# A 32-byte pad in front of the arena of a two-layer decoder trunk

## The chip, the cores and the metric

The kernel runs on one NeuronCore of one Trainium2 chip. The metric is the device time of one execution in microseconds (us), the median of several runs. The kernel before takes 2490.14 us (median of 3 runs, 2489.68 to 2490.35).

## What is computed

Two layers of a hybrid decoder trunk over 512 tokens of width 1024, all in float32. Each layer has three sub-layers with residual adds, each behind an RMSNorm: a parallel token mixing of four branches, a cross-attention with 4 heads into 256 memory tokens, and a gated MLP with a causal convolution of width 3. Cut to what matters:

```python
for l in range(DEPTH):                       # 2 layers
    h = rms_norm(x, mix_norm_g[l])
    seg_a, seg_b, seg_c, seg_d, seg_g = split_last(h @ w_in[l], SEGMENTS)   # 1024 x 9984
    y_a, y_b, y_c, y_d = dilated(seg_a), diff(seg_b), hgrn(seg_c), rwkv(seg_d)
    gates = jax.nn.sigmoid(seg_g.reshape(B, S, 4, D))
    merged = sum(gates[:, :, n] * (y_n @ p_n[l]))        # n = a, b, c, d
    x = x + merged @ w_mix_out[l]
    hq = rms_norm(x, mem_q_norm_g[l]) @ w_mem_q[l]
    kv = rms_norm(mem, mem_kv_norm_g[l]) @ w_mem_kv[l]
    p = jax.nn.softmax(hq @ k.T / 16)                    # 4 heads of 256
    x = x + (p @ v) @ w_mem_o[l]
    u = rms_norm(x, ffn_norm_g[l]) @ w_ffn_in[l]         # 1024 x 5632
    gate, val = jnp.split(causal_conv3(u), 2, axis=-1)
    x = x + (jax.nn.silu(gate) * val) @ w_ffn_out[l]     # 2816 x 1024
return rms_norm(x, final_norm_g)
```

## The kernel before, in words

**Numbers in two halves.** Every large product runs in fp32r, a float32 type of the matmul, with each operand cut into a rounded part (hi) and the rest (lo). One product of a 128x128 block is three matmuls that add up in PSUM (`mm3`): hi by hi, hi by lo, lo by hi. All of them are issued at L288, so the trace tells them apart by the names of their tiles. In a name like `ffn_pd<-xgh,whi`, `ffn_pd` is the PSUM tile written, the first name behind the arrow is the moving operand (streamed through the array) and the second is the stationary one (loaded ahead as weights, the LDWEIGHTS of the trace).

**Weights.** All weights come as 388 chunks of 128x1024 floats, 194 in each layer. `chunk` (from L473) loads one with a DMA from SP's queue into `wst`, rounds it to `whi` on ScalarE (L483) and subtracts on VectorE to get `wlo` (L484). There are 3, 4 and 4 buffers of these three.

**Kinds of fp32r matmul.** Four of them matter here:

- *weight-stationary, 512 columns* (`ws_tile`, `ws_run`): a 128x128 block of `whi` or `wlo` is stationary, 512 tokens of an activation move. 168 of a layer's 194 chunks are used so, with 8 blocks of 3 matmuls each: 2 x 168 x 24 = 8064 matmuls. They are the projections (`Cp_pd`, `Dp_pd`, `Bp_pd`, `A_pd`), the gates (`ga_pd` to `gd_pd`), the branch outputs (`pa_pd` to `pd_pd`), `mix_pd`, `mq_pd`, `mo_pd` and the MLP (`ffn_pd`). Per layer, the MLP has 66 chunks of them and `mix`, `mq` and `mo` 8 each, so that 2 x 90 x 24 = 4320 of the 8064 belong to these four.
- *weight-moving, 256 columns* (`tm_tile`): an activation is stationary and 256 columns of weights move: 18 chunks of each layer, four matmul rows of 128 tokens (two for `mv`), 1344 matmuls in all (`Cp_pd<-whi,xgh`, `Bp_pd<-whi,xgh`, `A_pd<-whi,xgh`, `mv_pd<-whi,mgh` and their lo forms).
- *memory keys, 256 columns* (`mk_pd`): weights stationary, 256 memory tokens moving, 384 matmuls.
- *cross-attention* (`matt_ps`): scores of 256 columns (`matt_ps<-mkh,mqh`, 192 matmuls) and the product of probabilities with values at 512 columns (`matt_ps<-mpth,mvh`, 96 matmuls). Here both operands are activations.

The other matmuls (mixers, transposes) are plain float32.

**Where the operands lie.** SBUF is cut into pools that lie one behind the other in each partition: `cp` (constants), `wp` (weights), `sp` (small and temporary tiles), `ar` (the arena). In the built program `cp` begins at byte 16512, `wp` at 33952, `sp` at 79008 and `ar` at 113792. Every buffer of `wp` (`wst`, `whi`, `wlo`) starts at a byte that is 32 above a multiple of 64, and so does every 128-column block of it, since a block is 512 bytes long. The arena has 15 slots of 4 KB and 25 of 2 KB and hands them out through `Arena.alloc`; 113792 is a multiple of 64, so every slot starts at byte 0 of a 64-byte line, and every block of 128 or 256 columns in it as well. All fp32r activations (`xgh`, `xgl`, `fh`, `fl`, `moh`, `mhh`, `mgh`, `mkh`, `mqh`, `mpth`, `mvh` and the like) lie in the arena, nearly all of `sp` at byte 32.

**Order of work.** `Weave` writes out, while the program is built, one fixed order for each engine: a queue of dense weight products, and chains of the mixers' steps that are put in between when a model of TensorE's time says that their inputs should be ready. `setup` (L607) runs first: it makes the constant `ones`, loads the first constants and `x`. The MLP has no chains beside it.

Of the kernel before, what the change touches and what calls it, by code (L numbers as in the profile page):

```python
# [9 lines left out]
F32 = mybir.dt.float32  # L10
# [11 lines left out]
P = 128  # L22
# [351 lines left out]
class Trunk:  # L374
# [232 lines left out]
    def setup(self):  # L607
        nc = self.nc
        self.ones = self.cp.tile([P, P], F32, name='ones')
        nc.vector.memset(self.ones, 1.0)  # L610
        nc.scalar.copy(self.ones[:, 0:2], self.ones[:, 2:4])
        self.load_cv(0)
        xg, acc = self.load_x()
        self.cst = self.cp.tile([P, NCS], F32, name='cst')
        nc.scalar.dma_start(self.cst, self.ins['cst'])
        return xg, acc
# [1385 lines left out]
```

## Time and profile before

| | before |
|---|---|
| median of 3 runs | 2490.14 us (2489.68 to 2490.35) |
| the profiled execution | 2490.42 us |
| its span, first to last instruction | 2488.6 us |
| TensorE matmul busy | 2439.0 us (98%), 13344 instructions |
| TensorE weight load busy | 1996.5 us (80%) |
| VectorE busy | 1513.4 us (61%) |
| ScalarE busy | 973.4 us (39%) |
| GpSimd busy | 455.6 us (18%) |
| mean granted TensorE clock | 0.995 of full speed |

Busy time is the union of an engine's instructions. A matmul's record in the trace is longer than the distance to the next one, because neighbours overlap: a 512-column matmul lasts some 0.40 us on record, but a new one starts every 0.23 us. What a stream of matmuls costs is therefore read from the starts, not from the mean duration.

### The profile page before, as it was taken

Reading aid. Unit: us, or ns where it says so; the run is one execution under the profiler, and the core shown is the slowest. Engines: PE = TensorE matmul, PEld = TensorE weight load, DVE = VectorE, ACT = ScalarE, POOL = GpSimd, SP = SyncE. Lnnn points to the kernel's source line nnn. Section 1 sums busy time; section 2 is a strip of 40 time slices with the busy share of each in tenths; the row PEclk is TensorE's granted clock in tenths of the full one; section 3 lists DMA queues with packets and bytes.
Section 4 is the critical chain, followed back from the end, with each engine's and each line's share of the span. In section 5 each row is a group of like instructions: output and inputs, shape, how many; then the busy total and the mean of one; then the engine's idle time right before and its main releaser. Section 6 shows DMA issues by size and latency. Waiting matters only on the chain.

```text
span 2488.6 us, 34307 instructions
## 1 busy us (share of the span) xinstructions
PE 2439.0 (98%) x13344; PEld 1996.5 (80%) x13344; DVE 1513.4 (61%) x2729; ACT 973.4 (39%) x1728; POOL 455.6 (18%) x374
## 2 busy tenths in 40 slices
PE   8999999999999999999999999999999999999997
PEld 7877887788889888888888788867888898888886
DVE  6787447756656566366466864387466565763762
ACT  6242524443334434234352335244333354432441
POOL 0220042244010111011102200433421001110112
PEclk9999999999999999999999999999999999999998
DMA  5224233224324122222322342332343332222221
GB/s 182 100 103 144 89 115 127 73 68 156 125 96 151 64 93 93 93 93 94 127 93 78 110 144 79 121 106 77 100 133 114 101 127 77 93 93 97 98 85 60
DMA packets 89602, 259.69 MB, mean 104 GB/s; under 512 B 18144, under 2 KB 21856, under 8 KB 89440
## 3 DMA queue, kind: packets, MB, share of 16 engines
q1 hardware_dynamic: 57168, 205.81, 25.0%
q10 hardware_dynamic: 25872, 30.58, 3.7%
q0 software_dynamic: 6400, 21.11, 2.7%
q8 instruction: 105, 1.72, 0.3%
q14 instruction: 57, 0.47, 0.1%
HBM read 234.32 MB, written 23.13 MB: 103 GB/s over the span
## 4 chain that ended last, share of the span: by engine, by line
PE 92%; DVE 5%; ACT 1%; issue 1%; DMA 1%; POOL 0%; DVEq 0%; ACTq 0%; SPq 0%
PE ffn_pd L288 30%; PE A_pd L288 7%; PE Bp_pd L288 5%; PE gc_pd L288 4%; PE Cp_pd L288 4%; PE gd_pd L288 4%; PE mq_pd L288 4%; PE mo_pd L288 4%; PE mix_pd L288 4%; PE ga_pd L288 4%; PE Dp_pd L288 3%; PE Db_ps L288 3%; PE gb_pd L288 2%; PE matt_ps L288 2%; PE mk_pd L288 2%; PE mv_pd L288 2%
## 5 line engine op out<-in xcount | busy, mean ns | idle before, releaser
L483 ACT CAST whi<-wst 128x1024 fp32r<-128x1024 f32 x388 | 405.3, 1049 | 830.5 <-PE ffn_pd L288 236.5
L484 DVE TENSOR_TENSOR wlo<-wst,whi 128x1024 fp32r<-128x1024 f32 x388 | 497.1, 1285 | 213.5 <-ACT whi L483 212.3
L288 PE MATMUL ffn_pd<-xgh,whi 128*128 128x512 f32 x704 | 278.8, 396 | 0.0
L288 PE MATMUL ffn_pd<-xgh,wlo 128*128 128x512 f32 x704 | 278.4, 395 | 0.0
L288 PE MATMUL ffn_pd<-xgl,whi 128*128 128x512 f32 x704 | 278.4, 395 | 0.0
L1866 POOL TENSOR_TENSOR ffn_ft<-ffn_ft,ffn_fc 128x512 f32<-128x512 f32 x44 | 60.1, 1366 | 563.0 <-DVE ffn_fu L1852 362.5
L288 PEld LDWEIGHTS ffn_pd<-xgh,wlo 128*128 128x128 f32 x704 | 132.2, 188 | 32.1
L288 PEld LDWEIGHTS ffn_pd<-xgl,whi 128*128 128x128 f32 x704 | 132.3, 188 | 31.9
L288 PEld LDWEIGHTS ffn_pd<-xgh,whi 128*128 128x128 f32 x704 | 132.3, 188 | 31.6
L288 PE MATMUL ffn_pd<-fh,wlo 128*128 128x512 f32 x352 | 139.2, 396 | 0.0
L288 PE MATMUL ffn_pd<-fh,whi 128*128 128x512 f32 x352 | 139.2, 396 | 0.0
L288 PE MATMUL ffn_pd<-fl,whi 128*128 128x512 f32 x352 | 139.2, 396 | 0.0
L288 PE MATMUL A_pd<-xgh,whi 128*128 128x512 f32 x256 | 106.9, 417 | 0.0
L288 PE MATMUL A_pd<-xgh,wlo 128*128 128x512 f32 x256 | 102.3, 399 | 0.0
L288 PE MATMUL A_pd<-xgl,whi 128*128 128x512 f32 x256 | 102.2, 399 | 0.0
L1853 DVE TENSOR_TENSOR ffn_fu<-ffn_pd,r_rbc 128x512 f32<-128x512 f32 x88 | 60.4, 688 | 57.6 <-PE ffn_pd L288 57.6
L531 DVE TENSOR_TENSOR fl<-ffn_ft,fh 128x512 fp32r<-128x512 f32 x44 | 30.5, 693 | 90.5 <-ACT fh L530 90.5
L530 ACT CAST fh<-ffn_ft 128x512 fp32r<-128x512 f32 x44 | 27.3, 621 | 144.1 <-POOL ffn_ft L1866 144.1
L1855 ACT ACTIVATE ffn_fc<-ffn_fu,cvt 128x512 f32<-128x512 f32 x88 | 71.7, 817 | 25.4 <-DVE ffn_fu L1853 25.4
L1415 POOL TENSOR_TENSOR A_rp<-A_rp,snr 128x512 f32<-128x512 f32 x24 | 50.4, 2098 | 167.4 <-DVE A_rp L1414 165.1
L288 PEld LDWEIGHTS ffn_pd<-fh,wlo 128*128 128x128 f32 x352 | 66.1, 188 | 16.1
L288 PEld LDWEIGHTS ffn_pd<-fl,whi 128*128 128x128 f32 x352 | 66.1, 188 | 16.0
(583 smaller groups left out, 6106.0 us busy)
## 6 DMA issues: line engine op xcount, KB each, us to landing
wst<-in_wst_dram SPq DMA_DIRECT2D x388, 512.0 KB, 3.5
gb_gate<-gb_gu ACTq DMA_DIRECT2D x16, 256.0 KB, 2.1
gd_gate<-gd_gu ACTq DMA_DIRECT2D x16, 256.0 KB, 2.1
gc_gate<-gc_gu ACTq DMA_DIRECT2D x16, 256.0 KB, 2.1
pc_gu<-gc_gate POOLq DMA_DIRECT2D x16, 256.0 KB, 3.6
pd_gu<-gd_gate POOLq DMA_DIRECT2D x16, 256.0 KB, 3.0
pb_gu<-gb_gate POOLq DMA_DIRECT2D x16, 256.0 KB, 3.1
x<-in_x_dram ACTq DMA_DIRECT2D x13, 256.0 KB, 3.4
```

The lines of the kernel that those rows point to most:

```text
L288: return self.te.matmul(out, lhsT, rhs, **kw)
L483: nc.scalar.copy(hi, st)
L484: nc.vector.tensor_sub(lo, st, hi.bitcast(F32))
L530: nc.scalar.copy(dst[0], src)
L531: nc.vector.tensor_sub(dst[1], src, dst[0].bitcast(F32))
L1415: nc.gpsimd.tensor_mul(t2, t2, self.snr)
L1853: nc.vector.tensor_mul(u[:, 2:514], ps, self.rb)
L1855: nc.scalar.activation(acc, u[:, 2:514], AF.Identity, scale=self.cv('cw2', ch), bias=self.cv('cb', ch))
L1866: nc.gpsimd.tensor_mul(th, th, cc[1])
```

## The change

A tile of 8 floats in each partition (32 bytes), `pad`, is taken from the pool `sp` before any other tile of it, and set to zero once on VectorE.

```diff
     def setup(self):
         nc = self.nc
         self.ones = self.cp.tile([P, P], F32, name='ones')
+        pad = self.sp.tile([P, 8], F32, name='pad')
+        nc.vector.memset(pad, 0.0)
         nc.vector.memset(self.ones, 1.0)
         nc.scalar.copy(self.ones[:, 0:2], self.ones[:, 2:4])
         self.load_cv(0)
```

In the built program every other tile of `sp` and every slot of `ar` lies 32 bytes higher than before, and no tile of `cp` or `wp` moves. The arena begins at byte 113824, so its slots start at byte 32 of a 64-byte line, as `wst`, `whi` and `wlo` do; nearly all of `sp` now starts at byte 0. The order of the instructions on every engine, and what each waits for, stay as they were, with one MEMSET of 128x8 more on VectorE at the very start.

## Rows read from the trace of the kernel before

**Rows 1.** The page: span, TensorE's busy time (share, instructions), granted clock in 40 slices.

```profile
span 2488.6 us, 34307 instructions
...
PE 2439.0 (98%) x13344; PEld 1996.5 (80%) x13344; DVE 1513.4 (61%) x2729; ACT 973.4 (39%) x1728; POOL 455.6 (18%) x374
...
PEclk9999999999999999999999999999999999999998
```

**Rows 2.** The page: shares by engine of the chain of work that ended last.

```profile
PE 92%; DVE 5%; ACT 1%; issue 1%; DMA 1%; POOL 0%; DVEq 0%; ACTq 0%; SPq 0%
```

**Rows 3.** Pieces of that chain in order of time: start us, us, what.

```profile
321.38 67.20 PE Bp_pd L288 x384
...
661.80 44.80 PE mix_pd L288 x192
...
753.18 22.72 PE mk_pd L288 x192
789.59 14.01 PE mv_pd L288 x120
...
883.25 358.39 PE ffn_pd L288 x1536
```

**Rows 4.** TensorE in order of time, MLP of layer 0: start us, us, operation.

```profile
1143.49 0.40 PE L288 MATMUL ffn_pd<-xgh,whi 128*128 128x512 f32 x1
1143.72 0.40 PE L288 MATMUL ffn_pd<-xgl,whi 128*128 128x512 f32 x1
1143.95 0.40 PE L288 MATMUL ffn_pd<-xgh,wlo 128*128 128x512 f32 x1
```

**Rows 5.** The same view, cross-attention of layer 0, probabilities by values.

```profile
803.43 0.40 PE L288 MATMUL matt_ps<-mpth,mvh 128*128 128x512 f32 x1
803.67 0.40 PE L288 MATMUL matt_ps<-mptl,mvh 128*128 128x512 f32 x1
803.90 0.39 PE L288 MATMUL matt_ps<-mpth,mvl 128*128 128x512 f32 x1
804.13 0.39 PE L288 MATMUL matt_ps<-mpth,mvh 128*128 128x512 f32 x1
...
806.17 0.28 PE L288 MATMUL matt_ps<-mkh,mqh 128*128 128x256 f32 x1
```

**Rows 6.** The same view, same place in layer 1.

```profile
2032.92 0.39 PE L288 MATMUL matt_ps<-mpth,mvh 128*128 128x512 f32 x1
...
2034.96 0.28 PE L288 MATMUL matt_ps<-mkh,mqh 128*128 128x256 f32 x1
```

**Rows 7.** The same view, scores of the cross-attention of layer 0.

```profile
826.13 0.28 PE L288 MATMUL matt_ps<-mkh,mqh 128*128 128x256 f32 x1
...
827.09 0.29 PE L288 MATMUL matt_ps<-mkh,mql 128*128 128x256 f32 x1
```

**Rows 8.** TensorE's waits: waiting line, releaser, us in total, times, longest.

```profile
PE Bb_ps L292 <- DVE bp L1497: 14.5, 13, 1.9
PE Cp_pd L288 <- ACT xgh L533: 9.8, 1, 9.8
PE Db_ps L292 <- DVE dsq L1048: 4.9, 2, 2.6
```

**Rows 9.** Groups of VectorE: line, operation, shapes, count, then busy us and mean ns.

```profile
L484 DVE TENSOR_TENSOR wlo<-wst,whi 128x1024 fp32r<-128x1024 f32 x388 | 497.1, 1285 | 213.5 <-ACT whi L483 212.3
L531 DVE TENSOR_TENSOR fl<-ffn_ft,fh 128x512 fp32r<-128x512 f32 x44 | 30.5, 693 | 90.5 <-ACT fh L530 90.5
L531 DVE TENSOR_TENSOR mhl<-mrg,mhh 128x512 fp32r<-128x512 f32 x16 | 10.7, 688 | 1.6 <-ACT mhh L530 1.4
L1852 DVE MEMSET ffn_fu<- 128x2 f32 x88 | 5.3, 60 | 0.0
```

**Rows 10.** Stretches: us, busy time (instructions) of PE, PEld, DVE, ACT, POOL, clock, DMA.

```profile
883.00:1241.60 358.60, 358.60 (x1540) 288.74 (x1539) 210.63 (x306) 133.94 (x168) 40.18 (x31) 1.00 0.31 101
```

## The prediction, made before the changed kernel was run

> **What bounds the kernel now.** I read the page first, then the chain of waits, then TensorE in order of time. The page shows TensorE busy for 2439.0 of 2488.6 us, at full clock (2.4 GHz) but for the last slice [rows 1], and 92% of the chain that ended last is TensorE [rows 2]. What it waits for is small: the three largest waits sum to 29 us [rows 8]. So the time is a number of matmuls times the distance between their starts, and a change that moves only addresses can act in one way that matters: by changing that distance.
>
> The chain gives the distance in long unbroken pieces. In the MLP, 1536 weight-stationary matmuls of 512 columns take 358.39 us, 233.3 ns each; `mix` gives the same, 44.80 us / 192 [rows 3]. That is 560 cycles of 2.4 GHz for 512 columns. The stretch of the MLP shows the other engines far from full: VectorE 210.6 and ScalarE 133.9 of 358.6 us, DMA 0.31 [rows 10]. Nothing else holds the stream there: TensorE paces itself.
>
> Now compare a stream of the same form whose two operands lie alike. In the cross-attention, probabilities by values, the moving `mpth`/`mptl` and the stationary `mvh`/`mvl` are both in the arena, at byte 0 of a 64-byte line; in the MLP the moving operand is at byte 0 and the stationary one at byte 32. After three matmuls in which it settles (starts 0.24, 0.23, 0.23 us apart), this stream runs nine steps from 804.13 to 806.17 us: 2.04/9 = 226.7 ns each, 544 cycles [rows 5]. Layer 1 repeats it, 2034.96 - 2032.92 = 2.04 us for nine [rows 6]. The record of one matmul is shorter too, 0.39 us against 0.40 [rows 4, 5]. Both streams have the pattern hi-hi, hi-lo, lo-hi, load the next stationary block during the matmul, and add into PSUM. What I see that differs is where the operands lie against each other.
>
> At 256 columns the picture turns. Weight-moving matmuls (moving at byte 32, stationary at 0) take 14.01/120 = 116.8 ns, memory keys (the other way round) 22.72/192 = 118.3 ns [rows 3]; scores, both in the arena, take (827.09 - 826.13)/8 = 120.0 ns [rows 7]. So unlike placement costs about the same whichever operand is shifted, and like placement costs 6.6 ns less at 512 columns and 1.7 to 3.3 ns more at 256. My theory: the reads of the next stationary block get in the way of the moving operand's reads, and how often depends on their offset against each other inside a 64-byte line, not on the byte itself.
>
> **The change, term by term.** It adds one MEMSET of 8 columns on VectorE; one of 2 columns takes 60 ns [rows 9]. It stands before all work, while `x` is still on its way and TensorE's first product waits 9.8 us for the first rounded block [rows 8]; were that cover gone, it would cost its 0.06 us or a little more. I cost it at nothing.
>
> It moves the arena from byte 0 to byte 32, the byte of the weights, so all fp32r matmuls become pairs that lie alike. No row shows a pair with both at byte 32. By my theory it costs what both at byte 0 costs. The bounds for a 512-column matmul: from below 226.7 ns, the fastest steady distance seen; from above today's distance plus twice what alike costs at 256 columns, 233.3 + 2 x 3.3 = 239.9 ns. I take 226.7, because that row has the same length and the same pattern.
>
> - Weight-stationary in the MLP, `mix`, `mq`, `mo`: 4320 x 6.6 ns = 28.5 us less. No chain of small steps runs beside the MLP, and VectorE would need 210.6 us in a stretch shortened to some 348 us [rows 10], so this is kept whole.
> - Weight-stationary in the mixing part: 3744 x 6.6 ns = 24.7 us less, but here chains of VectorE and ScalarE steps run beside the matmuls in a fixed order. Where a chain sets the end, faster matmuls only reach their wait earlier; late next is then the step that TensorE waits for today (`bp` at L1497, `dsq` at L1048 [rows 8]). 8% of the chain lies off TensorE already [rows 2], nearly all of it here, and more of it will once the matmuls shrink. I keep three quarters, 18.5 us; the ends are nothing and 24.7.
> - Weight-moving: 1344 x (120.0 - 116.8) = 4.3 us more; memory keys: 384 x 1.7 = 0.7 us more. The end on the other side: neither changes, 0.
> - Cross-attention: 288 matmuls that were alike and stay alike, 0. Plain float32 matmuls: I see no dependence on placement and take 0.
> - VectorE, ScalarE, GpSimd: `sp` against the arena was unlike and stays unlike. Subtractions from an `sp` tile (`fl`, unlike) and within the arena (`mhl`, alike) take 693 and 688 ns [rows 9], so a changed offset is worth 5 ns on an engine with room. 0.
> - DMA: the same transfers to rows shifted by 32 bytes. The weights' 388 transfers, most of the traffic, do not move. 0.
>
> Sum: -28.5 - 18.5 + 4.3 + 0.7 = -42.0 us. The profiled execution took 2490.4 us (a span of 2488.6 and 1.8 around it), which gives 2448.4; the median of the runs shown lies 0.3 lower, so I say **2448 us**. With all of the mixing part kept and nothing lost at 256 columns it is 2490.1 - 53.2 = 2437; with nothing kept in the mixing part, 2490.1 - 28.5 + 5.0 = 2467.
>
> **Rivals.**
>
> *No change: the two reads do not meet.* Then the distance is set by the number of columns and by the place in the program, the nine fast steps have another reason (another PSUM tile, groups of 6 matmuls and not of 24), and the 8064 matmuls stay at 233.3 ns: 2490 us, at most 2495 if the 256-column ones still go to 120 ns. For it: only two runs of nine steps show the fast distance, and no row shows both operands at byte 32. Against it: the three settling matmuls are of the same form and PSUM tile as the nine, and scores sit at 120.0 where the unlike kinds sit below. The Trainium skill stands with this rival: SBUF - State Buffer, "Who interferes with whom", gives TensorE two independent read ports, one for the moving operand and one for the weight load, and says that it waits on nobody, and under "Specifications" it has lines of 16 bytes, of which a shift by 32 bytes is two whole ones. By that rule the time would stay at 2490. The traces disagree so far: 226.7 against 233.3 ns for matmuls of one shape.
>
> *Slower: the reads fall into step the bad way.* If alike means that the two streams keep their phase, that phase can be the one in which they always meet, as the scores seem to have it: 120.0 against 116.8 ns. If the 8064 matmuls lock as the scores do, in proportion to their length, they go to 239.9 ns: 8064 x 6.6 = 53 us more, with 5.0 at 256 columns 2548 us. It decides as soon as the distance rises by 0.6 ns (8064 x 0.6 = 5 us). Against it: the nine steps have just this length and locked the good way, both times.
>
> *Given back: the chains take it.* The matmuls reach 226.7 ns, but the mixing part keeps next to nothing and 256 columns cost more: 2465 to 2485 us. For it: the order is fixed and was laid out for today's distances. Against it: waits of some 30 us in 2489 [rows 8].
>
> That the pad might not shift the arena is no rival: the addresses of the built program are shown above.
>
> **How the numbers follow.** Forecast (2432 to 2465) 0.60; given back 0.08; no change 0.20; slower 0.12. A measurement of this kernel can tell about 0.2%, 5 us, from no change. So faster 0.68, within 0.2% 0.20, slower 0.12. The range reaches from 2434 (all kept, 256 columns a little better than today) to 2493: it takes in the forecast, what is given back and most of no change, and leaves out the slower rival and the outermost ends, less than 2 in 10. The forecast's own range is 2434 to 2465.
>
> **What would show it.** Right: the MLP's piece of 1536 matmuls falls from 358.4 to about 348.2 us with records of 0.39 us, `mix` from 44.8 to 43.5, while `mk` (192) rises from 22.7 to 23.0 and the weight-moving kinds to 120 ns a matmul; TensorE's waits grow by some us in the mixing part. Wrong: the MLP's piece stays at 358 us (no change), or goes towards 368 us (slower). If it falls and the whole does not, the waits of TensorE in the mixing part must have grown by the difference.

## The result, and the profile after

The changed kernel takes **2450.47 us** (median of 4 runs, 2449.37 to 2452.40) against 2489.91 us of the kernel before beside it (median of 4): a ratio of 0.9844, 95% interval 0.9831 to 0.9856. The forecast was 2448 us, with a stated range of 2434 to 2493.

The page of the changed kernel, its span, busy times, and the shares of the chain of waits, stands against [rows 1, 2]:

```profile
span 2447.6 us, 34308 instructions
...
PE 2396.2 (98%) x13344; PEld 1999.2 (82%) x13344; DVE 1511.7 (62%) x2730; ACT 974.1 (40%) x1728; POOL 457.2 (19%) x374
...
PE 92%; DVE 5%; ACT 1%; issue 1%; DMA 0%; POOL 0%; DVEq 0%; ACTq 0%; SPq 0%
```

The span is 41.0 us shorter and TensorE's busy time 42.8 us, while VectorE, ScalarE and GpSimd are busy as before within 2 us and the shares of the chain are the same within 1%. So the bound did not move to another engine: the same matmuls follow each other faster. The long pieces of the chain say how much, one by one, against [rows 3]:

```profile
318.48 66.55 PE Bp_pd L288 x384
...
653.49 43.63 PE mix_pd L288 x192
...
742.48 23.03 PE mk_pd L288 x192
779.33 14.39 PE mv_pd L288 x120
...
872.21 348.20 PE ffn_pd L288 x1536
```

`ffn_pd` goes from 358.39 to 348.20 us, 348.20/1536 = 226.7 ns a matmul; `mix_pd` gives 227.2 ns. `mk_pd` goes up, 23.03/192 = 119.9 ns, and so does `mv_pd`, 14.39/120 = 119.9 ns. Up at 256 columns and down at 512: a change of the clock would move both the same way, and the mean granted clock is 0.995 of full speed in both executions. Whether it is the placement of the operands is what the experiments test.

TensorE's waits, against [rows 8]:

```profile
PE Bb_ps L292 <- DVE bp L1499: 15.1, 14, 1.9
PE Cp_pd L288 <- ACT xgh L533: 9.8, 1, 9.8
PE Db_ps L292 <- DVE dsq L1050: 5.1, 2, 2.8
```

All ten lines of that view sum to 40.6 us, before to 39.2. The chains of small steps took back next to nothing.

The starts of the same pieces split the 41.0 us by stage. In both kernels the first product starts 9.8 us into the span, so what a stage gained is the difference of its ends less that of its starts: 8.3 us in the mixing part of layer 0 (`mix_pd` starts at 661.80 before, at 653.49 after), 2.7 from there to the MLP's long piece (883.25, 872.21), 10.2 in that piece. Layer 1 repeats it with 6.9, 2.7 and 10.2.

### The profile page after: what moved, and what is told of

Same layout as the page of the kernel before. It is cut to its first block, busy times and chain, and to the rows that moved or that the text cites. A ratio compares the mean times of both kernels' runs of the same rounds, so it can differ in the third digit from the quotient of the medians.

```text
span 2447.6 us, 34308 instructions
## 1 busy us (share of the span) xinstructions
PE 2396.2 (98%) x13344; PEld 1999.2 (82%) x13344; DVE 1511.7 (62%) x2730; ACT 974.1 (40%) x1728; POOL 457.2 (19%) x374
## 4 chain that ended last, share of the span: by engine, by line
PE 92%; DVE 5%; ACT 1%; issue 1%; DMA 0%; POOL 0%; DVEq 0%; ACTq 0%; SPq 0%
PE ffn_pd L288 29%; PE A_pd L288 7%; PE Bp_pd L288 5%; PE Cp_pd L288 4%; PE gd_pd L288 4%; PE mo_pd L288 4%; PE mq_pd L288 4%; PE mix_pd L288 4%; PE ga_pd L288 4%; PE gc_pd L288 4%; PE Dp_pd L288 3%; PE Db_ps L288 3%; PE gb_pd L288 2%; PE matt_ps L288 2%; PE mv_pd L288 2%; PE mk_pd L288 2%
## 5 line engine op out<-in xcount | busy, mean ns | idle before, releaser
L575 POOL TENSOR_TENSOR mo_sqa<-mo_sqa,mo_sqt 128x512 f32<-128x512 f32 x14 | 23.6, 1686 | 297.8 <-ACT mo_sqa L571 257.9
```

The costliest lines, as they stand in the source:

```text
L575: (eng or nc.gpsimd).tensor_add(acc[:, :n], acc[:, :n], t[:, :n])
```

## The experiments

In what follows the **offset** of a pair is the start of the stationary block minus the start of the moving operand, in bytes, modulo 256. For weight-stationary matmuls and `mk_pd` it is the place of the weights less that of the arena; for weight-moving ones (`mv_pd`) it has the other sign. Before, 512 columns and `mk_pd` are at 32 and `mv_pd` at 224 (= -32); the changed kernel has all of them at 0. Two theories stood at the start: the offset decides, or something else that the pad moved does (the arena's own byte, or `sp`).

**1. The pad in the constants' pool.** The weights move with the arena, so only the offset is undone.

```diff
-        pad = self.sp.tile([P, 8], F32, name='pad')
+        pad = self.cp.tile([P, 8], F32, name='pad')
```

> The pad is taken from the pool of the constants and not from sp, so that the weights move too: arena at byte 32 and sp at byte 0 as in the changed kernel, whi and wlo at byte 0, unlike the arena again. If the offset between the two operands decides: 1536 MLP matmuls take 358 us (233.3 ns each), mk 22.7 us, total 2490 us. If a moving operand at byte 32 is fast in itself, or if the shift of sp brings the gain: 348 us and 2450 us.

Measured: 2489.97 us (median of 8), ratio to the kernel before 0.9996 (0.9985 to 1.0007). Its pieces of the chain:

```profile
753.06 22.73 PE mk_pd L288 x192
789.46 14.01 PE mv_pd L288 x120
883.10 358.41 PE ffn_pd L288 x1536
```

Each piece is back at its value before, within 0.02 us, although the arena lies at byte 32, `sp` at byte 0 and the MEMSET is there. So none of these three makes the gain; what this run took back is the place of the weights against the arena.

**2 to 4. The weights alone moved, by 32, 16 and 48 bytes.** No pad; `whi` and `wlo` are cut from buffers 64 bytes longer, beginning 8, 4 or 12 floats in.

```diff
-            hi = self.wp.tile([P, 1024], F32R, tag='whi', bufs=self.wb[1], name='whi%d' % n)
-            lo = self.wp.tile([P, 1024], F32R, tag='wlo', bufs=self.wb[2], name='wlo%d' % n)
+            hi = self.wp.tile([P, 1040], F32R, tag='whi', bufs=self.wb[1], name='whi%d' % n)[:, 8:1032]
+            lo = self.wp.tile([P, 1040], F32R, tag='wlo', bufs=self.wb[2], name='wlo%d' % n)[:, 8:1032]
```

> No pad; whi and wlo alone lie 32 bytes higher in slightly larger buffers, at byte 0 of a line, like the arena at byte 0; sp and the arena keep their bytes. If the offset decides: MLP piece 348 us, mk 23.0 us, total 2450 us, as with the pad. If the moving operand's byte or the shift of sp decides: 358 us, 2490 us. If two operands at byte 0 are better still than two at byte 32 (whole lines), under 348 us.

> No pad; whi and wlo 16 bytes higher, at byte 48, so that the stationary operand lies 48 bytes above the moving one inside a 64-byte line. If only equal bytes help: 358 us for the MLP piece, total 2490 us. If the cost grows with the distance on the 64-byte circle (16 here, 32 before): halfway, some 353 us and 2470 us. If 32 bytes is the unit that counts, 16 bytes could look like 0 (348 us) or like 32 (358 us).

> No pad; whi and wlo 48 bytes higher, at byte 16, 16 above the moving operand. The mirror of the run with 16 bytes: the same time as that one if the cost is symmetric in who leads, another one if it matters which of the two reads comes first to a line. Equal bytes only: 358 us for the MLP piece, 2490 us.

Measured: 2474.36 us with 32 bytes (ratio 0.9934, 0.9911 to 0.9956), 2474.14 with 16 (0.9939, 0.9916 to 0.9961), 2485.53 with 48 (0.9981, 0.9970 to 0.9993). With 32 bytes both operands are at byte 0 of a 64-byte line, and the theory asked for 348 us:

```profile
748.40 22.35 PE mk_pd L288 x192
784.49 14.18 PE mv_pd L288 x120
877.92 354.55 PE ffn_pd L288 x1536
```

The MLP's piece keeps 6 us too much: a miss, and the useful one. The longer buffers are 4160 bytes apart, 65 times 64, so the eight of them lie at eight different multiples of 64 to the arena, where the kernel before has all its buffers 4096 bytes apart, at one offset. Sorted by the offset of the next stationary block (addresses of the built program beside the starts in the trace, distances over 260 ns left out), the 512-column matmuls of this one run average:

| offset | 0 | 64 | 128 | 192 |
|---|---|---|---|---|
| mean distance of starts, ns | 228.5 | 233.3 | 232.7 | 229.3 |

So equal bytes of a 64-byte line are not enough, and 64 bytes is the wrong unit. Offsets 256 bytes apart look more alike: 227.9 and 228.8 ns at 0 and 256 modulo 512, 233.2 and 233.4 at 64 and 320, 232.9 and 232.3 at 128 and 384, with 228.7 and 230.5 at 192 and 448 the widest pair. The runs with 16 and 48 bytes mix four offsets in the same way (48, 112, 176, 240 and 16, 80, 144, 208 modulo 256; their MLP pieces take 354.70 and 357.26 us), so their totals can't be held against their expectations, which took one offset for granted.

**5 to 9. Pads of 64 to 288 bytes.** To have one offset in a run, the pad itself is varied; weights and their buffers stay as in the kernel before.

```diff
-        pad = self.sp.tile([P, 8], F32, name='pad')
+        pad = self.sp.tile([P, 72], F32, name='pad')
```

with 72, 24, 56, 16 and 40 floats: 288, 96, 224, 64 and 160 bytes.

> Pad of 288 bytes: arena 256 bytes further than in the changed kernel, still at byte 32 of a 64-byte line; stationary minus moving is 256 modulo 512. The run with weights at byte 0 in larger buffers mixed offsets (multiples of 64) and showed about 228 ns at 0 and 256 modulo 512, and 229 to 233 ns at the other multiples. If the unit is 64 bytes or 256 bytes: MLP piece of 1536 matmuls 348 us, total 2450 us. If it is 512 bytes or more: 353 us or above, total over 2470 us.

> Pad of 96 bytes: arena at byte 32 of a 64-byte line as in the changed kernel, offset 448 (192 modulo 256). If equal bytes of a 64-byte line are what counts (the theory of the prediction): 348 us, total 2450 us. If the unit is 256 bytes: the mixed run had 229 to 231 ns there, MLP piece 351 to 355 us, total 2460 to 2475 us, with mk some 114 to 115 ns a matmul (22.0 us for 192).

> Pad of 224 bytes: again byte 32 of a 64-byte line, offset 320 (64 modulo 256). 64-byte theory: 348 us, total 2450 us. 256-byte unit: the mixed run had 233 ns there, MLP piece 358 us, mk 113.7 ns (21.8 us for 192), weight-moving kinds 116 ns; total 2485 to 2490 us.

> Pad of 64 bytes: arena at byte 0 of a 64-byte line, unlike the weights as in the kernel before, offset 480 (224 modulo 256, or -32). 64-byte theory: as before, 358 us, total 2490 us. 256-byte unit: between the mixed runs at 208 (232 ns) and 240 (227.7 ns), some 230 ns, 353 us, total 2470 us; it also tells whether +32 and -32 cost the same.

> Pad of 160 bytes, the last multiple of 64 that is missing: byte 32 of a 64-byte line as in the changed kernel, offset 384 (128 modulo 256). 64-byte theory: 348 us, total 2450 us. 256-byte unit: the mixed run had 232.6 ns there for 512 columns, 118 ns for mk and 119 for weight-moving; MLP piece 357 us, total 2486 us.

The chain of waits, first for the pad of 288 bytes (offset 0 again):

```profile
742.45 23.03 PE mk_pd L288 x192
779.30 14.39 PE mv_pd L288 x120
872.12 348.20 PE ffn_pd L288 x1536
```

96 bytes (offset 192):

```profile
745.23 22.61 PE mk_pd L288 x192
781.25 13.62 PE mv_pd L288 x120
873.73 351.59 PE ffn_pd L288 x1536
```

224 bytes (offset 64):

```profile
752.34 21.78 PE mk_pd L288 x192
787.78 14.13 PE mv_pd L288 x120
881.54 358.40 PE ffn_pd L288 x1536
```

64 bytes (offset 224):

```profile
752.73 22.40 PE mk_pd L288 x192
788.82 14.20 PE mv_pd L288 x120
882.65 358.40 PE ffn_pd L288 x1536
```

160 bytes (offset 128; in layer 1 the MLP's piece of this run takes 356.96 us, the only one of the five that differs between the layers by over 0.1 us):

```profile
752.13 22.78 PE mk_pd L288 x192
788.62 14.23 PE mv_pd L288 x120
882.38 358.39 PE ffn_pd L288 x1536
```

Divided by their counts, and with the kernel before and the changed one, these pieces give the distance of starts for every pair as a function of its own offset (for `mv_pd` that is the negative of the column's offset in its run, so its numbers come from other runs than those of `mk_pd`):

| offset modulo 256 | 0 | 32 | 64 | 128 | 192 | 224 |
|---|---|---|---|---|---|---|
| 512 columns, `ffn_pd`, ns | 226.7 | 233.3 | 233.3 | 233.3 | 228.9 | 233.3 |
| 256 columns, `mk_pd`, ns | 119.9 | 118.3 | 113.4 | 118.6 | 117.8 | 116.7 |
| 256 columns, `mv_pd`, ns | 119.9 | 118.3 | 113.5 | 118.6 | 117.8 | 116.8 |
| total of the run with the weights there, us | 2450 | 2490 | 2489.86 | 2489.19 | 2456.89 | 2490.39 |

Three things are to be seen. First, the pads of 96, 224 and 160 bytes leave weights and arena at the same byte of a 64-byte line, and cost 2457, 2490 and 2489 us (ratios 0.9873, 1.0000 and 0.9998 to the kernel before): the 64-byte theory falls. The pad of 288 bytes gives 2450.09 us (median of 2; 0.9846, 0.9817 to 0.9874): a step of 256 bytes brings the whole gain back and no smaller step tried does, so 256 bytes are the unit. Second, `mk_pd` and `mv_pd`, weights standing in one and moving in the other, agree within 0.1 ns at every offset of this table: it is the difference of the two starts that counts, not which operand lies where (that 64 has a second distance shows in experiment 10). Third, the best offset depends on the length: 0 for 512 columns, and 64 for 256 where its lower distance comes about. Both then reach the same distance per column, 226.7/512 = 113.4/256 = 0.443 ns.

The expectation for 64 bytes (2470 us, from neighbours in the mixed run) missed: 2490 us, no gain. Smaller ones missed too: with 96 bytes `mk_pd` ran at 117.8 ns for 114 to 115 and the total came 3 us below its range, and with 224 bytes `mv_pd` ran at 117.8 for 116. A rise or fall between two measured offsets is not to be read as a slope.

**10 and 11. A place for each kind of matmul, and the changed kernel again.** The buffers of `whi` and `wlo` are 256 bytes longer, so that all eight keep one offset, and a chunk begins at float 0 for weight-moving matmuls, 32 for `mk` and 16 for the rest; the pad is 96 bytes. The lines below stand in `open`, `chunk`, `tm_chunks` and `setup`.

```diff
+        self.off = 32 if name == 'mk' else 16
-    def chunk(self):
+    def chunk(self, o=None):
+        o = self.off if o is None else o
-            hi = self.wp.tile([P, 1024], F32R, tag='whi', bufs=self.wb[1], name='whi%d' % n)
-            lo = self.wp.tile([P, 1024], F32R, tag='wlo', bufs=self.wb[2], name='wlo%d' % n)
+            hi = self.wp.tile([P, 1088], F32R, tag='whi', bufs=self.wb[1], name='whi%d' % n)[:, o:o + 1024]
+            lo = self.wp.tile([P, 1088], F32R, tag='wlo', bufs=self.wb[2], name='wlo%d' % n)[:, o:o + 1024]
-        return [self.chunk(), self.chunk()]
+        return [self.chunk(0), self.chunk(0)]
-        pad = self.sp.tile([P, 8], F32, name='pad')
+        pad = self.sp.tile([P, 24], F32, name='pad')
```

> The weights get a place for each kind of matmul, inside buffers 256 bytes longer: weight-stationary 512 columns at offset 0 modulo 256 to the moving operand, weight-moving 256 columns and memory keys at offset 64 (stationary above moving). If each kind keeps the distance it had in the run that suited it: MLP piece 348.2 us, mk 192 in 21.8 us, mv 120 in 13.6 us; against the changed kernel 1344 x (120.3 - 113.5) + 384 x (120.0 - 113.4) = 11.7 us less, total 2439 us, if the mixing part keeps all of it, 2442 us with three quarters. If the distance depends on something else than the offset modulo 256 (the byte of one operand): no gain, 2450 us or worse.

> The changed kernel once more, beside the version with three places: 2450 us, MLP piece 348.2 us.

Measured, on one chip: 2443.00 us (median of 5, ratio to the kernel before 0.9816, 0.9802 to 0.9829) against 2450.29 us for the changed kernel (0.9841, 0.9827 to 0.9854). It beats both kernels, the changed one by 7.3 us, where 8 to 12 were expected; by the starts of the two profiled executions, weight-moving matmuls give 4.5 us of it and `mk_pd` 0.8, and the rest is no more than the 4 us by which runs of the changed kernel differ. The chain of waits of the version with three places:

```profile
317.95 66.13 PE Bp_pd L288 x384
...
741.55 22.61 PE mk_pd L288 x192
777.56 13.62 PE mv_pd L288 x120
869.63 348.20 PE ffn_pd L288 x1536
```

`mv_pd` reaches 113.5 ns as foreseen and the MLP keeps its 348.20 us. But `mk_pd`, at the same offset of 64, runs at 117.8 ns here and ran at 113.4 with the pad of 224 bytes. The weight-moving matmuls of `Bp_pd` do the same: less 192 at 226.7 ns, 66.13 us leave 22.6 us for 192, 117.8 ns. The pad of 96 bytes had shown the same inside one kernel, with `Bp_pd`'s weight-moving half at offset 64 in both layers:

```profile
319.38 65.73 PE Bp_pd L288 x384
...
1531.88 66.56 PE Bp_pd L288 x384
```

Less 192 at 228.9 ns, layer 0 leaves 21.8 us for 192, 113.4 ns, and layer 1 leaves 22.6, 117.8 ns. So offset 64 has two steady distances at 256 columns, and the offset alone doesn't tell which one a stream falls into. What does (how the stream is entered, or higher bits of the addresses, would be guesses) was not tried.

## Why the prediction was right, and where not

**What bounds the kernel: right.** Only addresses moved, and the time went down by what the distance of starts gave. The "full clock" of [rows 1] was read too finely, since a 9 there means 90% or more; but the mean granted clock is 0.995 before and after, so the clock can't make the gain.

**Both operands at byte 32 cost what both at byte 0 cost: right.** The nine fast steps of the cross-attention [rows 5, 6] had 226.7 ns, and the MLP now has 226.7 ns. At offset 0 the arena lay at byte 128 modulo 256 in those steps, at 160 in the changed kernel and at 224 in the version with three places, always with the same distance.

**"Depends on their offset against each other inside a 64-byte line": half wrong.** The offset against each other is right (the pad in the constants' pool); the 64-byte line is not. The unit is 256 bytes, and of the five pads that make the bytes of a 64-byte line equal (32, 96, 160, 224 and 288 bytes) two gain all, one less and two nothing. The rows could have said so: all pairs I had called alike were alike modulo 512 as well, and I read the smallest unit into them. That the sum did not suffer was luck: a pad of 32 bytes brings the offset to 0 in every unit.

**The terms.** Measured by the starts of every matmul in the two traces, paired one by one:

| term | forecast, us | measured, us |
|---|---|---|
| 512 columns in MLP, `mix`, `mq`, `mo` | -28.5 | -27.7 |
| 512 columns in the mixing part | -18.5 | -18.3 |
| weight-moving, 256 columns | +4.3 | +4.1 |
| `mk`, 256 columns | +0.7 | +0.6 |
| plain float32, cross-attention | 0 | +0.1 |

**The quarter lost in the mixing part: right in size, wrong in cause.** I gave it to the chains, whose waits were to grow. Of the 24.7 us that all 3744 matmuls could give, 18.3 came, and the waits grew by 1.4 us. Most of the other 5 us is a stream settling, so the size came out by luck. After each burst of float32 matmuls the next half dozen run nearly as before. A block of 21 matmuls of `Dp_pd` between two bursts, in the chain of waits, before:

```profile
72.81 5.09 PE Dp_pd L288 x21
```

and after:

```profile
71.75 4.99 PE Dp_pd L288 x21
```

21 matmuls at 6.6 ns less would be 0.14 us; 0.10 us came. TensorE in order of time, at the beginning and the end of that block after the change (start us, us, operation), shows where the rest stayed:

```profile
72.02 0.39 PE L288 MATMUL Dp_pd<-xgl,whi 128*128 128x512 f32 x1
72.25 0.40 PE L288 MATMUL Dp_pd<-xgh,wlo 128*128 128x512 f32 x1
...
73.18 0.39 PE L288 MATMUL Dp_pd<-xgh,whi 128*128 128x512 f32 x1
...
76.35 0.39 PE L288 MATMUL Dp_pd<-xgh,wlo 128*128 128x512 f32 x1
```

Five steps from 72.02 to 73.18 take 232 ns each, the next fourteen to 76.35 take 3.17/14 = 226.4. Over the mixing part, distances over 260 ns left out, the first six fp32r matmuls behind an interruption went from 232.6 to 231.1 ns (685 of them), the later ones from 233.3 to 227.1 (2674). At 6.6 ns each the first six should have given 4.5 us and gave 1.0. I had seen this settling in the cross-attention and left it out of the sum.

**The rival "no change"** had its strongest support in the rule of the Trainium skill, SBUF — State Buffer, "Who interferes with whom", by which TensorE reads its moving operand and its weights through two independent ports and waits on nobody. The runs disagree: the same matmuls, reading the same amounts, start every 226.7 or every 233.3 ns by nothing but the offset of the two operands. The measurement decides. The other reasons that this rival gave for the nine fast steps, the PSUM tile and the groups of 6 matmuls, fall with it: `ffn_pd` kept both its tile and its groups, and went to 226.7 ns.

**The rival "slower"**, that the streams lock the bad way, did not come true at 512 columns: no offset tried was slower than the 233.3 ns before by more than 0.1 ns. At 256 columns it is what happens at offset 0, 119.9 ns against 118.3 and 116.8 before, as the sum had it.

That the reads of the next stationary block get in the way of the moving operand's is still an argument, not a finding: the runs show that the offset of the two decides, with a period of 256 bytes, and that a stream settles over some matmuls. The records of the loads give no sign of it at 512 columns: those of `ffn_pd` last 188 ns on average in both kernels, while the distance between its matmuls fell by 6.6 ns; those of `mk_pd`, which became slower, went from 188 to 192 ns. Every fp32r matmul here loads its own block, so a stream without loads wasn't tried.

## What to carry to other kernels

Where TensorE is busy throughout, read the distance between the starts of equal matmuls, not their mean duration, and compare it between streams of one shape: 6.6 ns of 233.3 hid in 8064 matmuls and were worth 1.6% of the kernel, settling and the loss at 256 columns taken off. Before a placement is copied from a fast stream, all its addresses should be compared at more than one unit, and the placement swept: here a pad of 32 or 288 bytes gains 40 us, 96 gains 33, and 64, 160 or 224 gain nothing. Buffers that rotate should lie a multiple of 256 bytes apart, or each has its own offset.

## What was not expected

- The distance of fp32r matmuls repeats with 256 bytes of offset between stationary and moving operand, and the best offset differs by length: 0 at 512 columns (226.7 against 233.3 ns), 64 at 256 columns (113.4 against 119.9 at 0), where a stream falls into the lower of its two distances.
- At offset 64, 256-column streams have two steady distances, 113.4 and 117.8 ns, in one and the same run, and even for the same tile in the two layers (`Bp_pd` with the pad of 96 bytes).
- After an interruption by float32 matmuls about six 512-column matmuls pass before the fast distance sets in (232 ns, then 226.4).
